# Recurrence of a hybrid block on one core: the next group's triangular inverse moved to a lower priority band, and another order and length of the filling projections

## The chip, the cores and the metric

The kernel runs on 1 core of one Trainium2 chip. The time is device microseconds (us) from launch to end, the median of several runs; lower is better. Engines are named as the profile names them: PE (TensorE), DVE (VectorE), ACT (ScalarE), POOL (GpSimd), SP (SyncE, which here only issues DMAs).

## The reference

Two layers of a block over 512 latent tokens and 256 context tokens, width 1024. In each layer one input projection of the normalised tokens feeds three mixers: a bidirectional RWKV-7 recurrence, multi-head latent attention, and windowed grouped-query attention (gqa). Each is multiplied by its own SiLU gate, projected, merged by sigmoid gates and passed through an output projection. The recurrence, as the reference states it:

```
def step(S, inp):
    r_t, w_t, k_t, v_t, kk_t, a_t = inp
    sa = jnp.einsum('bhvk,bhk->bhv', S, kk_t)
    S = (S * w_t[:, :, None, :] - sa[..., None] * (kk_t * a_t)[:, :, None, :]
         + v_t[..., None] * k_t[:, :, None, :])
    return S, jnp.einsum('bhvk,bhk->bhv', S, r_t)
```

It runs over 768 tokens, 8 heads of 64 channels, in both directions.

## The kernel before

**The recurrence.** It is done in chunks of 64 tokens: 12 steps, each of which handles 8 heads in both directions (16 pairs). Within a chunk the token-by-token rule becomes a triangular system, so each chunk needs the inverse of a unit lower triangular 64x64 matrix per pair. These inverses are made for a group of four steps at a time (`NS` 4, `NG` 3 groups; `rwkv_inverse`, L634-685). The matrices are loaded (tile TT, L641/642, issued on SP), turned with a stream transpose (L647), and the two 32x32 diagonal blocks are inverted on DVE by 30 pairs of a multiply (L657) and an add (L659), then turned back (L662, L663). PE then makes the block below the diagonal from two halves of matmuls: zp, yp, zp, yp. Of the tile TT and of its working tile `inv` there is one buffer each; of the result YB there are two.

A step (`rwkv_step`, L687-742) is a chain: PE makes Rp, ACT copies it, PE makes Up with the inverse, ACT and DVE copy it (L708, L709), PE makes Sp, DVE makes the new state So (L719, L720), which ACT and DVE copy for the next step (L694, L695). The scores of the chunk two steps ahead (`rwkv_scores`, L587-633: matmuls scps, DVE masks L623 and L625) are woven into the step, in two halves.

**The filling.** Since the chain leaves PE idle, the remaining tiles of the input projection are woven in. A tile is 128 output columns over eight blocks of 128 input channels; in single precision each product is three matmuls (`hh`x`wh`, `hl`x`wh`, `hh`x`wl`), for 512 latent tokens and, in layer 0, for 256 context tokens too. It is cut into 8 pieces; `pace(n)` emits n of them. `FILL` (L33) holds, per layer, how many stand before the first inverse, during it, in its last parts, and in the steps. The matmul results lie in two PSUM buffers (`g`, GB 2). A "raw" tile is copied out by ACT (L756); a "silu" tile (a gate) is evacuated by ACT's tanh (L758) and a DVE multiply (L760), both at the band SERVE. In layer 0 the woven work carries pieces of the next conditioning vectors along (modps, modpt; DVE L261, L269).

**What sets the order.** The program is emitted under priority bands, and a scheduler gives each engine one fixed order: SERVE first, then B+1 (steps, scores, inverses), B+3 (gqa tokens), B+4 (filling). PE's instructions of the recurrence and its filling are chained to the order in which they were written (`in_line`, L146-160). In the loop over steps the next group's inverse is a generator, `ahead`: one part of its DVE work after each of steps 0, 1 and 2 of a group, its matmuls within step 3.

Of the kernel before, what the change touches and what calls it, by code (L numbers as in the profile page):

```python
# [29 lines left out]
GB, RB, CB = 2, 3, 2  # L30


FILL = ((48, 36, 2, (2, 2, 2), (3, 3, 3), 2), (72, 56, 4, (2, 2, 2), (3, 3, 3), 2))  # L33

QUEUES = (("scalar", "sync", "sync", "scalar"), ("sync", "scalar", "sync", "sync"))

# [1 line left out]
NS, NG = 4, 3  # L38
# [22 lines left out]
def build(tc, A, out):  # L61
# [13 lines left out]
    @contextmanager  # L75
    def band(b):

        keep, mine = tc.cur_priority, bands.get(b, b * 1000000)
        tc.cur_priority = mine
        yield  # L80
        bands[b] = tc.cur_priority
        tc.cur_priority = keep
# [64 lines left out]
    @contextmanager  # L147
    def in_line():
        line["on"] = True
        yield  # L150
        line["on"] = False
# [339 lines left out]
    def rwkv(l, D, last, DL, B, pace, zlast):  # L491

        with tc.tile_pool(name="rw", bufs=1, reuse_waits="tile") as rp:
            yo = rp.tile([P, 4, T], F32, name="yo")
            st = {"seen": set(), "S": None}
            parts, YB = {}, {}

            def scores(i):
                if i < NCH:
                    parts[i] = yield from rwkv_scores(l, last, rp, i)  # L500

            def invert(g):
                if g < NG:
                    YB[g] = rp.tile([P, 32, 64], F32, tag="YB", name="YB", bufs=2)
                    yield from rwkv_inverse(l, rp, g, YB[g])

            def rest(*gens):
                for g in gens:
                    for _ in g:
                        pass  # L510

            with band(B + 1):
                rest(scores(0), scores(1))
                ahead = invert(0)
                for _ in range(3):
                    next(ahead)
            with band(B + 4), tc.issue_after(zlast):
                pace(FILL[l][1])
            with band(B + 1), in_line():
                for _ in ahead:  # L520
                    pace(FILL[l][2])
                ahead = out = iter(())
                for i in range(NCH):
                    if i % NS == 0:
                        rest(ahead)
                        ahead = invert(i // NS + 1)
                    nxt = scores(i + 2)
                    step = rwkv_step(l, last, i, yo, st, DL, rp, parts.pop(i), YB[i // NS])
                    for n in FILL[l][3 if i % NS < NS - 1 else 4]:
                        next(step, None)  # L530
                        next(nxt, None)
                        if i % NS == NS - 1:
                            next(ahead, None)
                        next(out, None)
                        pace(n)
                    rest(step, nxt)
                    if i % NS < NS - 1:
                        next(ahead, None)
                    if i in READY and (i > 3 or not last):
                        rest(out)  # L540
                        out = readout(l, D, rp, yo, READY[i])
                for _ in out:
                    pace(FILL[l][5])

    def readout(l, D, rp, yo, part):

        b, t = part

        def cols(a):
            a = a.rearrange("p (b t) -> p b t", t=T // 2)[:, b, t]  # L550
            return a if len(a.shape) == 3 else a.unsqueeze(1)

        def like(a, y):
            return a.rearrange("p (b t) -> p b t", b=y.shape[1])

        tmp = rp.tile([P, 6, 256], F32, tag="AR", name="ro", bufs=4)
        def spread(p):
            ps = psum_bcast(256)
            mm(ps, bones, tmp[:, 4 + p % 2])
            V.tensor_scalar(tmp[:, p], ps, 1.0 / 64, None, ALU.mult)  # L560

        for p in range(4):
            y = cols(yo[:, p])
            ps = psum_bcast(256)
            mm(ps, C["center"], y)
            S.copy(y, like(ps, y))
            S.activation(like(tmp[:, 4 + p % 2], y), y, AF.Square)
            if p:
                spread(p - 1)
            yield  # L570
        spread(3)
        var = tmp[:, 0:4]
        S.activation(var, var, AF.Ln, bias=b_gn)
        S.activation(var, var, AF.Exp, scale=-0.5)
        for p in range(4):
            y = cols(yo[:, p])
            ro = rp.tile([P, 2, 256], F32, tag="UV", name="ro2", bufs=4)
            bv, gt = like(ro[:, 0], y), like(ro[:, 1], y)
            DMA.dma_start(bv, cols(bv_d[l][p]))
            DMA.dma_start(gt, cols(g_d[l][p]))  # L580
            V.scalar_tensor_tensor(y, y, D["gng"][:, p:p + 1], like(tmp[:, p], y), ALU.mult, ALU.mult)
            V.scalar_tensor_tensor(y, y, D["gnb"][:, p:p + 1], bv, ALU.add, ALU.add)
            V.scalar_tensor_tensor(y, gt, 0.5, y, ALU.mult, ALU.mult)
            DMA.dma_start(cols(yg_d[l][p]), y)
# [160 lines left out]
    def proj(l, hh, hl, j, dst, segs, kind, side):  # L745

        t = spool.tile([P, T], F32, tag="st", name="st", bufs=2)
        if j == T_KR:
            ps = yield from narrow_steps(A["w_in"][l][j], KT, hh, hl, segs, side)
        else:  # L750
            ps = yield from gemm_steps(A["w_in"][l][j], KT, hh, hl, segs, "gg", side)
        with band(SERVE):
            for (s0, n), p in zip(segs, ps):
                sl = slice(s0, s0 + n)
                if kind == "raw":
                    S.copy(t[:, sl], p)  # L756
                else:
                    S.activation(t[:, sl], p, AF.Tanh, scale=0.5)  # L758
                    if kind == "silu":
                        V.scalar_tensor_tensor(t[:, sl], t[:, sl], 1.0, p, ALU.add, ALU.mult)  # L760
            s0 = segs[-1][0]
            DMA.dma_start(dst[:, s0:T], t[:, s0:T])
# [653 lines left out]
    for l in range(2):  # L1416
        last = l == 1
# [3 lines left out]
        B = 10 * l  # L1421
# [22 lines left out]
        def tiles():  # L1444

            zb = [(T_CQ + j, zb_d[l][j], (LAT,) if last and j < 2 else BOTH, "raw") for j in range(4)]
            zc = [(T_ZC + j, zb_d[l][4 + j], (LAT,) if last and j < 4 else BOTH, "raw") for j in range(6)]
            ga, gb, gc = ([(t + j, g_d[l][4 * n + j], segs, "silu") for j in range(4)]
                          for n, t in enumerate((T_GA, T_GB, T_GC)))
            todo = zb[2:] + zc[4:] + zc[:4] + zb[:2] + ga + gb if last else zb + ga + gb + zc  # L1450
            todo += gc + [(T_ZG + j, th_zg[l][j], segs, "tanh") for j in range(24)]
            for a in todo:
                yield from proj(l, hh, hl, *a, side)
                yield

        steps = tiles()

        def pace(n):

            for _ in zip(range(n), steps):  # L1460
                pass
# [3 lines left out]
        with band(B + 4):  # L1465
            pace(FILL[l][0])
        ss = cpool.tile([P, 6, 10], F32, tag="ss", name="ss")
        if last:
            cctx.close()
            with band(B + 3):  # L1470
                gqa_tokens(l, F, last, ss)
        rwkv(l, D, last, DL, B, pace, zlast)
        weights["queue"] = getattr(nc, QUEUES[l][2])
        with band(B + 4), tc.issue_after(line["last"]):
            pace(22 * 8 - sum(FILL[l][0:2]) - 2 * FILL[l][2] - NG * (3 * sum(FILL[l][3]) + sum(FILL[l][4])) - 4 * FILL[l][5])

# [162 lines left out]
```

## Time and profile before

| | us |
|---|---|
| median of 3 runs (lowest to highest) | 2433.22 (2431.24 to 2439.78) |
| profiled execution | 2433.78 |
| span of its trace | 2432.1 |
| PE busy | 2166.8 (89%) |
| DVE busy | 1278.8 (53%) |
| ACT busy | 894.1 (37%) |
| POOL busy | 844.3 (35%) |

The span runs from the first to the last instruction of the trace; 1.7 us of the execution lie around it. Times in the trace count from the span's start. Layer 0's recurrence takes from about 325 us to 675, layer 1's from about 1650 to 1945. A busy share is an average over all of the kernel; within the recurrence PE and DVE take turns at being waited for.

### The profile page before, as it was taken

The page shows a single profiled execution, that of the slowest core. Times are in us where ns is not written, and L with a number is a line of the kernel's source. Part 1 is how long each engine was busy: PE and PEld are TensorE (multiplying, and loading weights), DVE is VectorE, ACT ScalarE, POOL GpSimd, SP SyncE. Part 2 cuts the span into 40 slices and gives each one's busy share as a digit, 9 for nine tenths or more (in the row PEclk, how much of TensorE's full clock was granted, in tenths as well). Part 3 has the DMA queues.
Part 4 walks back from the last instruction along what each step waited for, and adds up shares of the span by engine and source line. Part 5 has one row for each costly group of instructions (what it writes and reads, how often), then busy time and mean ns, then how long its engine had stood idle before and what let it go on. Part 6 is the DMA issues. An engine that isn't in the chain of part 4 may idle for free. (4 is left out here: it accounts for less than half of the span.)

```text
span 2432.1 us, 42833 instructions
## 1 busy us (share of the span) xinstructions
PE 2166.8 (89%) x16824; PEld 1657.7 (68%) x16824; DVE 1278.8 (53%) x2300; ACT 894.1 (37%) x1654; POOL 844.3 (35%) x699
## 2 busy tenths in 40 slices
PE   7988895888998999899989998798968998999989
PEld 4766683667877666766767786666756876666667
DVE  5466326865347663466145356736577456545223
ACT  4443221223354333543222345332322465334322
POOL 1244221111123444444333224443211144454464
PEclk9998997998999999999999999899988999999989
DMA  7146665445251013511685314665553262011474
GB/s 251 61 137 195 199 198 129 127 127 140 73 176 50 20 53 95 172 36 47 217 269 172 122 61 125 180 194 160 134 124 88 90 208 87 18 52 36 139 248 159
DMA packets 330442, 314.25 MB, mean 129 GB/s; under 512 B 112768, under 2 KB 239488, under 8 KB 330240
## 3 DMA queue, kind: packets, MB, share of 16 engines
q1 hardware_dynamic: 315120, 283.97, 39.2%
q10 hardware_dynamic: 15120, 27.53, 3.5%
q8 instruction: 133, 2.18, 0.4%
q14 instruction: 69, 0.57, 0.1%
HBM read 213.64 MB, written 97.78 MB: 128 GB/s over the span
## 5 line engine op out<-in xcount | busy, mean ns | idle before, releaser
L166 POOL TENSOR_TENSOR wl<-wf,wh 128x512 fp32r<-128x512 f32 x316 | 426.1, 1350 | 1060.1 <-ACT wh L165 979.9
L154 PE MATMUL g<-hh,wh 128*128 128x512 f32 (+1 forms) x1264 | 467.1, 370 | 14.1 <-DVE st L760 11.2
L154 PE MATMUL g<-hh,wl 128*128 128x512 f32 (+1 forms) x1264 | 457.0, 362 | 1.5 <-POOL wl L166 1.5
L154 PE MATMUL g<-hl,wh 128*128 128x512 f32 (+1 forms) x1264 | 454.1, 359 | 0.0
L165 ACT CAST wh<-wf 128x512 fp32r<-128x512 f32 x316 | 195.2, 619 | 503.4 <-PE g L154 233.8
L154 PEld LDWEIGHTS g<-hh,wh 128*128 128x128 f32 x1264 | 247.8, 196 | 66.4 <-issue 14.9
L154 PEld LDWEIGHTS g<-hh,wl 128*128 128x128 f32 x1264 | 247.7, 196 | 43.0 <-issue 9.4
L154 PEld LDWEIGHTS g<-hl,wh 128*128 128x128 f32 x1264 | 248.7, 197 | 38.7 <-issue 10.1
L867 POOL TENSOR_TENSOR acc<-acc,pe 128x512 f32<-128x512 f32 (+2 forms) x128 | 146.3, 1143 | 144.6 <-ACT pe L863 135.0
L863 ACT ACTIVATE pe<-stp 128x256 f32<-128x256 f32 (+2 forms) x224 | 114.5, 521 | 201.7 <-PE stp L154 194.9
L845 DVE TENSOR_REDUCE mx<-mps 128x1 f32<-128x384 f32 (+2 forms) x256 | 127.8, 535 | 68.7 <-PE mps L154 66.4
L154 PE MATMUL yps<-pe,vh 128*64 128x256 f32 (+1 forms) x704 | 132.5, 386 | 0.0
L154 PE MATMUL g<-yh,wh 128*128 128x512 f32 (+1 forms) x224 | 84.8, 384 | 21.9 <-DVE zt L1349 11.0
L1349 DVE SCALAR_TENSOR_TENSOR zt<-zt,g 128x512 f32<-128x512 f32 (+1 forms) x56 | 32.0, 576 | 129.8 <-PE g L154 86.6
L659 DVE TENSOR_TENSOR YB<-YB,inv 128x30 f32<-128x30 f32 (+9 forms) x180 | 91.9, 511 | 5.3
L657 DVE TENSOR_TENSOR inv<-inv,YB 128x30 f32<-128x30 f32 (+9 forms) x180 | 87.8, 488 | 8.9 <-issue 2.8
L154 PE MATMUL g<-yl,wh 128*128 128x512 f32 (+1 forms) x224 | 85.2, 384 | 6.3 <-POOL yl L1334 6.2
L154 PE MATMUL gc<-hh,wh 128*128 128x512 f32 x192 | 79.1, 412 | 7.8 <-ACT hh L325 4.5
L758 ACT ACTIVATE st<-g 128x256 f32<-128x256 f32 (+1 forms) x108 | 56.6, 524 | 76.0 <-PE g L154 66.4
L623 DVE TENSOR_TENSOR AR<-scps,cst 64x256 f32<-64x256 f32 x96 | 40.1, 418 | 82.2 <-PE scps L154 81.1
L154 PE MATMUL g<-yh,wl 128*128 128x512 f32 (+1 forms) x224 | 82.1, 371 | 0.0
L154 PE MATMUL gc<-hl,wh 128*128 128x512 f32 x192 | 79.5, 414 | 0.0
(395 smaller groups left out, 4402.0 us busy)
## 6 DMA issues: line engine op xcount, KB each, us to landing
wf<-w_in SPq DMA_DIRECT2D x159, 256.0 KB, 3.0
wf<-ada_w SPq DMA_DIRECT2D x96, 256.0 KB, 3.7
wf<-w_in ACTq DMA_DIRECT2D x81, 256.0 KB, 3.0
bkd<-bk SPq DMA_DIRECT2D x16, 768.0 KB, 5.2
zt<-thzg SPq DMA_DIRECT2D x48, 256.0 KB, 3.8
wf<-w_bo SPq DMA_DIRECT2D x40, 256.0 KB, 3.3
thzg<-st SPq DMA_DIRECT2D x24, 384.0 KB, 2.3
md<-zt SPq DMA_DIRECT2D x32, 256.0 KB, 3.5
```

The lines of the kernel that those rows point to most:

```text
L154: queued(TE.matmul(o, l, r, start=start, stop=stop, **kw))
L165: S.copy(wh, w32)
L166: eng.tensor_tensor(wl, w32, wh.bitcast(F32), ALU.subtract)
L623: V.tensor_tensor(AR[oth, pds, 2 * par, :], ps[oth, :, a0:a0 + 64], msk("ms", oth), ALU.mult)
L657: V.tensor_tensor(t3, M3[:, 0:j, j:j + 1].to_broadcast([P, j, n]), Y3[:, j:j + 1, j + 1:32].to_broadcast([P, j, n]), ALU.mult)
L659: V.tensor_tensor(Y3[:, 0:j, j + 1:32], Y3[:, 0:j, j + 1:32], t3, ALU.add)
L758: S.activation(t[:, sl], p, AF.Tanh, scale=0.5)
L845: V.tensor_reduce(mx, ps, AX.X, ALU.max)
L863: S.activation(e, st, AF.Exp, scale=scale)
L867: G.tensor_tensor(acc, keep.pop(0, acc), e, ALU.add)
L1349: V.scalar_tensor_tensor(th, th, 1.0, p_, ALU.add, ALU.mult)
```

## The change

Three edits. The next group's inverse is started at the group's first step, all of its DVE work at once, in a band of its own (B+2) between the steps and the filling; the calls that did a part after each step go. In layer 0 the six copied tiles `zc` come right after the four `zb`, ahead of the gates `ga` and `gb`. And the pieces of filling during the first inverse grow from 36 to 64 in layer 0 and from 56 to 60 in layer 1.

```diff
-FILL = ((48, 36, 2, (2, 2, 2), (3, 3, 3), 2), (72, 56, 4, (2, 2, 2), (3, 3, 3), 2))
+FILL = ((48, 64, 2, (2, 2, 2), (3, 3, 3), 2), (72, 60, 4, (2, 2, 2), (3, 3, 3), 2))
...
                 for i in range(NCH):
                     if i % NS == 0:
                         rest(ahead)
+
                         ahead = invert(i // NS + 1)
+                        with band(B + 2):
+                            for _ in range(3):
+                                next(ahead, None)
...
                     rest(step, nxt)
-                    if i % NS < NS - 1:
-                        next(ahead, None)
...
-            todo = zb[2:] + zc[4:] + zc[:4] + zb[:2] + ga + gb if last else zb + ga + gb + zc
+            todo = (zb[2:] + zc[4:] + zc[:4] + zb[:2] if last else zb + zc) + ga + gb
```

Lines of the changed kernel stand 2 further down in these functions (L647 is L649, L663 is L665, L760 is L762).

DVE, layer 0, where the inverse of the second group begins. Before, it begins right after the state of step 0 (So, UV) and the masks of a later step's scores (L623, L625) come in between its pairs:

```order
L722 TENSOR_TENSOR So<-Sp,DL 128x512
L695 COPY UV<-So 64x512
L647 STREAM_TRANSPOSE inv<-TT 128x1024
L760 SCALAR_TENSOR_TENSOR st<-st,g 128x512
L261 COPY row<-modps 128x256
L653 MEMSET YB 128x32
L657 TENSOR_TENSOR inv<-inv,YB 128x30
L659 TENSOR_TENSOR YB<-YB,inv 128x30
```

Now it begins after the first masks within step 3 (the So and UV ahead of them are those of step 2):

```order
L722 TENSOR_TENSOR So<-So,DL 128x512
L697 COPY UV<-So 64x512
L741 TENSOR_TENSOR yo<-yo,Yp 128x4x64 x2
L762 SCALAR_TENSOR_TENSOR st<-st,g 128x512
L625 TENSOR_TENSOR AR<-scps,cst 64x4x64
L627 TENSOR_TENSOR TR<-scps,cst 128x4x64
L625 TENSOR_TENSOR AR<-scps,cst 64x4x64
L627 TENSOR_TENSOR TR<-scps,cst 128x4x64
L649 STREAM_TRANSPOSE inv<-TT 128x1024
L655 MEMSET YB 128x32
L659 TENSOR_TENSOR inv<-inv,YB 128x30
L661 TENSOR_TENSOR YB<-YB,inv 128x30
```

All 30 pairs then follow one another with nothing between them, up to the two transposes, and the copy of step 3's Up comes behind. What has moved is the whole inverse, from steps 0 to 2 into step 3; layer 1's stands alike, with 24 operations of gqa's tokens (three sets for q, three for k) among its pairs. On SP the last two of the four loads of TT for this group, which stood ahead of the loads for the scores of step 3, now stand behind those of BK for step 7.

PE in step 3 of layer 0, first before, then now: zp, which reads the inverse, is the third thing in the step in both.

```order
L154 MATMUL Rp<-UV,AR 64x64 x16
L154 MATMUL scps<-AR,BK 128x128 x8
L154 MATMUL zp<-inv,TT 32x32 x32
L154 MATMUL g<-hh,wh 128x256
L154 MATMUL g<-hl,wh 128x256
L154 MATMUL g<-hh,wl 128x256
```

```order
L154 MATMUL Rp<-UV,AR 64x64 x16
L154 MATMUL scps<-AR,BK 128x128 x8
L154 MATMUL zp<-inv,TT 32x32 x32
L154 MATMUL g<-hh,wh 128x256
L154 MATMUL g<-hl,wh 128x256
L154 MATMUL g<-hh,wl 128x256
```

PE's order around zp has not moved; what stands on DVE ahead of the result that it reads has.

DVE in layer 0's first inverse, its end. Before, the pairs run out without a gate's evacuation between them:

```order
L657 TENSOR_TENSOR inv<-inv,YB 128x58
L659 TENSOR_TENSOR YB<-YB,inv 128x2x29
L657 TENSOR_TENSOR inv<-inv,YB 128x30
L659 TENSOR_TENSOR YB<-YB,inv 128x30
L662 STREAM_TRANSPOSE YB<-YB 128x32x32
L663 STREAM_TRANSPOSE inv<-YB 128x1024
L760 SCALAR_TENSOR_TENSOR st<-st,g 128x512
```

Now the evacuations (L762) of the third gate tile stand at the very end, one within the last pair and one behind the transposes, and the fourth's behind those:

```order
L661 TENSOR_TENSOR YB<-YB,inv 128x2x29
L659 TENSOR_TENSOR inv<-inv,YB 128x30
L762 SCALAR_TENSOR_TENSOR st<-st,g 128x256
L661 TENSOR_TENSOR YB<-YB,inv 128x30
L664 STREAM_TRANSPOSE YB<-YB 128x32x32
L665 STREAM_TRANSPOSE inv<-YB 128x1024
L261 COPY row<-modps 128x256
L762 SCALAR_TENSOR_TENSOR st<-st,g 128x512
L272 TENSOR_TENSOR mod_162<-modpt,pp 128x4
L762 SCALAR_TENSOR_TENSOR st<-st,g 128x256
```

The first two gate tiles' evacuations stand after the 7th, after the 10th, in the 18th and after the 20th pair; PE has 3.5 tiles more ahead of the first zp than before.

## Rows read from the trace of the kernel before

**Rows 1.** The page: the span, and the busy time of each engine.
```profile
span 2432.1 us, 42833 instructions
PE 2166.8 (89%) x16824; PEld 1657.7 (68%) x16824; DVE 1278.8 (53%) x2300; ACT 894.1 (37%) x1654; POOL 844.3 (35%) x699
```

**Rows 2.** Waits of PE, 370 to 425 us: us in total, times, longest.
```profile
PE zp L154 <- DVE inv L663: 29.7, 1, 29.7
```

**Rows 3.** Timeline of DVE, layer 0's first inverse: start, duration, operation, [idle before].
```profile
372.61 2.01 DVE L647 STREAM_TRANSPOSE inv<-TT 128x1024 f32<-128x1024 f32 x1
...
380.29 0.41 DVE L760 SCALAR_TENSOR_TENSOR st<-st,g 128x256 f32<-128x256 f32 x1
...
394.96 0.55 DVE L657 TENSOR_TENSOR inv<-inv,YB 128x234 f32<-128x234 f32 x1
...
408.99 1.25 DVE L663 STREAM_TRANSPOSE inv<-YB 128x1024 f32<-128x1024 f32 x1
```

**Rows 4.** Timeline of PE, the first zp of two groups.
```profile
410.29 1.92 PE L154 MATMUL zp<-inv,TT 32*32 32x32 f32 x64 [29.73 <-DVE inv L663]
...
490.42 1.20 PE L154 MATMUL zp<-inv,TT 32*32 32x32 f32 x64
```

**Rows 5.** Windows: stretch, length; busy PE, PEld, DVE, ACT, POOL; PEclk, DMA, GB/s.
```profile
400.00:420.00 20.00, 9.71 (x222) 7.76 (x223) 11.29 (x23) 6.19 (x9) 3.02 (x3) 0.63 0.17 50
...
1180.00:1190.00 10.00, 6.54 (x18) 4.48 (x18) 0.00 (x0) 3.38 (x7) 6.63 (x7) 0.66 0.83 259
```

**Rows 6.** Timeline of DVE: evacuations of two gate tiles that follow each other.
```profile
357.47 0.42 DVE L760 SCALAR_TENSOR_TENSOR st<-st,g 128x256 f32<-128x256 f32 x1 [2.58 <-ACT st L758]
...
367.52 0.42 DVE L760 SCALAR_TENSOR_TENSOR st<-st,g 128x256 f32<-128x256 f32 x1 [2.56 <-ACT st L758]
```

**Rows 7.** Timeline of PE, layer 0: Rp of steps 0, 3, 4, 8 and 9.
```profile
421.82 1.15 PE L154 MATMUL Rp<-UV,AR 128*64 128x64 f32 x32
...
486.94 1.98 PE L154 MATMUL Rp<-UV,AR 128*64 128x64 f32 x32
...
513.98 1.15 PE L154 MATMUL Rp<-UV,AR 128*64 128x64 f32 x32
...
613.42 1.15 PE L154 MATMUL Rp<-UV,AR 128*64 128x64 f32 x32
...
628.63 1.09 PE L154 MATMUL Rp<-UV,AR 128*64 128x64 f32 x30
```

**Rows 8.** Timeline of DVE: last mask of the first half of step 0's scores.
```profile
425.21 0.41 DVE L625 TENSOR_TENSOR TR<-scps,cst 128x256 f32<-128x256 f32 x1
```

**Rows 9.** Timelines of SP's queue and of DVE: the second group's load, what waits for it.
```profile
432.05 0.56 SPq L642 DMA_DIRECT2D TT<-ttd  x1
...
487.69 0.59 SPq L592 DMA_DIRECT2D BK<-bkd  x1
...
435.92 2.01 DVE L647 STREAM_TRANSPOSE inv<-TT 128x1024 f32<-128x1024 f32 x1 [1.41 <-DMA TT<-ttd]
```

**Rows 10.** Timeline of PE, layer 1: Rp of steps 0, 1, 4; zp in step 3.
```profile
1731.00 1.15 PE L154 MATMUL Rp<-UV,AR 128*64 128x64 f32 x32
...
1741.71 1.15 PE L154 MATMUL Rp<-UV,AR 128*64 128x64 f32 x32
...
1790.54 1.92 PE L154 MATMUL zp<-inv,TT 32*32 32x32 f32 x64 [13.83 <-DVE inv L663]
...
1809.84 1.15 PE L154 MATMUL Rp<-UV,AR 128*64 128x64 f32 x32
```

**Rows 11.** Lines of DVE, 1650 to 1990 us, gqa's tokens: xcount | busy, mean ns | idle before.
```profile
L1166 DVE TENSOR_REDUCE ss<-x 128x2 f32<-128x128 f32 (+1 forms) x10 | 4.4, 442 | 15.5 <-ACT x L1165 15.4
L1140 DVE TENSOR_TENSOR rp<-gqm,scq 128x256 f32<-128x256 f32 x8 | 3.0, 413 | 0.0
L1136 DVE TENSOR_TENSOR x<-gqm,ccq 128x512 f32<-128x512 f32 x4 | 2.8, 691 | 0.5 <-DVE ss L1166 0.4
L1140 DVE TENSOR_TENSOR rp<-gqm,sck 128x64 f32<-128x64 f32 x8 | 1.5, 214 | 0.0
```

## The prediction

> **What bounds the kernel now.** I began with the page's busy times [rows 1]: PE at 89% is the engine that fills the span, so outside the recurrence nothing here can move much. Next, PE's waits by stretch. The largest single one in the recurrences is in layer 0: the first zp waits 29.7 us for the first inverse [rows 2]. The timelines show why. DVE starts that inverse at 372.61 and is done at 410.24 (408.99 and 1.25) [rows 3], PE ran out of filling at 380.56 (410.29 less 29.73) [rows 4]. Some 36 us of the 37.6 are the inverse itself, the rest other small operations: this is the price of an inverse that DVE does in one piece.
>
> The second inverse of layer 0 is the opposite case: begun at 435.92 [rows 9], spread over steps 0 to 2, and finished in time, so that its zp at 490.42 carries no wait [rows 4]. It costs something all the same: from Rp of step 0 to Rp of step 4 pass 92.2 us (421.82 to 513.98), where step 8, with no inverse beside it, takes 15.2 [rows 7]. In layer 1 the same stretch takes 78.8 us (1731.00 to 1809.84) against 10.7 for step 0, and there zp in step 3 waits 13.8 [rows 10].
>
> **The change part by part.** The sum is made against the profiled execution, 2433.8, which is 0.6 above the median of the runs.
>
> *Layer 0's first inverse.* The change puts 28 more pieces, 3.5 tiles, ahead of the first zp. A tile with its riders takes 10.05 us here (357.47 to 367.52) [rows 6], so PE has 35 us for a hole of 29.7, and if nothing else were in the way, all of the hole would go. Something is. Four of the tiles there are now gates, whose results leave PSUM by DVE, in DVE's fixed order among the pairs, and PE has two buffers. Before, the same tile that is now the first gate had its context half evacuated at 380.29 [rows 3]; the next one's is ready 10 us later, near 390.5. Its place on DVE, though, is in the 18th pair (394.96 before), so with the two evacuations ahead of it about 397, and PE, ready for the third gate at about 391.5, loses some 6 us. The third's place is in the last pair: 407 plus four evacuations, about 409 to 410. The fourth can't begin before that, and its second half not before the evacuation behind the transposes, about 415. PE is then at zp near 425, with 35 us more done than before at 410.3: it lost 10 to 12 us on the way, where it lost 29.7. I take 11. To this comes the slow restart: after the wait zp took 1.92 us, elsewhere 1.20 [rows 4], and the granted clock in 400 to 420 was 0.63 [rows 5]; I put that at 2. Gain 29.7 - 11 + 2 = **21**; bounds 32 (no such coupling) and 10 (it costs twice as much).
>
> *Layer 0, second inverse.* The lower band doesn't lay it between the steps. By the order, none of its DVE work comes before the masks in step 3, then all of it comes in one piece, and zp on PE is right behind. PE then has nothing it may do. Steps 0 to 2 go undisturbed, 15.2 each, 45.5 in all. In step 3 the masks end 3.8 us after Rp (425.21 + 0.41 against 421.82) [rows 7, 8], then 36 us of inverse, then what followed zp before, 23.6 (490.42 to 513.98). One more wait: the inverse needs TT. SP's queue got to the loads for the next scores about 0.8 us into step 3 (487.69), and the last load of TT landed some 5.4 us after its issue at 432.05 (DVE waited for it until 435.92, an estimate of 3.9 for issue and landing) [rows 9]; the last two loads of TT are now queued behind those, so I add 4 us (0 to 8). Sum 45.5 + 3.8 + 4 + 36 + 23.6 = 112.9, against 92.2: **+21** (13 to 27). The restart at half clock is in it only as far as it was before (Rp of step 3 took 1.98 instead of 1.15).
>
> *Layer 1, second inverse.* The same, with gqa's three q and three k sets on DVE among the pairs. A set of each is two reductions of 0.44, 0.69 and 0.29 for the products, two times 0.41 and two times 0.21 [rows 11] (the 0.29 is an estimate: a little under 0.69 x 0.21/0.41), 3.1 us, three times 9.4. Steps 0 to 2: 3 x 10.7, and 1 for gqa there, 33. Step 3: 3.8 + 1 for TT + 36 + 9.4 + 19.3 (1790.54 to 1809.84, which has the slow clock in it) = 69.5. Together 102.5 against 78.8: **+24** (14 to 30).
>
> *Third inverses.* They begin within step 4 instead of just ahead of it, mixed with the steps' own work as before, since by then the steps are held by the readout and by the masks. Same DVE work, same steps beside it: 0 in layer 0 (-4 to 4), +2 in layer 1 (0 to 4).
>
> *The rest.* Copies ahead of gates take DVE work from before the first inverse to among its pairs, which is priced above; ACT, at 37% [rows 1], does either kind. The gates that the first readout reads are done 116 pieces in, 112 are needed, so no wait there. Layer 1's four further pieces stand where PE had work anyway: 0. Where layer 0's filling ends, fewer pieces are left, and the merge's first matmuls now come before gqa's last; in 1180 to 1190 PE was busy 6.54 of 10 us at a clock of 0.66 [rows 5], so -4 (-8 to 0).
>
> Sum: -21 + 21 + 24 + 0 + 2 - 4 = +22, that is 2455.8; less the 0.6 to the median, **2455 us**.
>
> A rule that bears on the clock term: the Trainium skill, "TensorE: Matmul & The Clock Gate", section "HAM oscillation — how this bites in real kernels", says that an engine that falls idle between bursts pays a cold start at each return. By it the change swaps one such return for another: layer 0's first inverse loses its own, step 3 gains one, and the 2 us credited above would be given back; the sum would be 24 instead of 22. The trace agrees that the return is slow (1.92 against 1.20), and doesn't show what a wait in step 3 of layer 0 does.
>
> **The rivals.**
>
> *Faster: the band does what it says in the last groups.* If steps 4 to 7 run first and the third inverse fills their holes only, these steps, 99.4 us from Rp of step 4 to that of step 8 (513.98 to 613.42) [rows 7], come down toward 3 x 15.2 + 23.6 = 69.2. That is 30 us in layer 0, and layer 1's group, an estimate from the same ratio, 20. With all of it the sum is 22 - 50 = -28, 2405; it decides for faster from 30 of the 50 on. For it: the inverse begins later than before, after step 4's masks. Against it: DVE's work between step 4 and step 7 is the same, and the steps on PE need DVE's masks and copies that stand behind the pairs.
>
> *Within 0.3%: the first hole goes entirely and the lumps cost less.* If evacuations find DVE in time (-32), TT lands early (+17) and gqa's sets slip into the wait without lengthening it (+15), the sum is -32 + 17 + 15 + 2 - 4 = -2, 2431. For it: a hole of 29.7 for 35 us of filling. Against it: PSUM has two buffers and DVE one order.
>
> *Slower still.* PE loses in the first inverse twice what I took (-10), the TT loads come at the late end (+27), layer 1's chain of gqa waits for its transposes on a PE that stands at zp (+30): -10 + 27 + 30 + 4 = +51, 2484.
>
> *That the change does nothing where it says so* would need an order like before; the order shows the inverses moved, so this holds only if the steps wait for something else at the same places. It ends with the second rival.
>
> **How the numbers follow.** The forecast has 0.62 (its own range 2442 to 2468, all slower), the faster rival 0.13, the same-time rivals 0.16, the slower still 0.09. What a measurement here tells from no change is about 0.3%, 7.3 us: 2425.9 to 2440.5. So slower 0.62 + 0.09 = 0.71, within 0.16, faster 0.13. The range of 8 in 10 leaves out most of the faster rival and of the slower one: 2428 to 2474.
>
> **What would show it.** In the profile after: in layer 0 the wait of the first zp for L665 shrunk to a few us, with waits of the filling's g for L762 in its place, 6 to 12 us in all; in step 3 of layer 0 a wait of zp for L665 of about 37 to 41 us, and in layer 1 of 40 to 50; steps 0 to 2 at about 15 and 11 us; the clock at 0.6 or so behind both waits; the stretch of steps 4 to 7 within 4 us of 99. The forecast is wrong if these two waits are not there or are under 25 us each, if steps 4 to 7 come down by more than 10 us, or if the first inverse's gain is given back by its evacuations.

## The result and the profile after

The changed kernel takes 2489.76 us (2486.84 to 2492.06, 4 runs) against 2434.3 before (2431.24 to 2439.78, 4 runs): a ratio of 1.0236, 95% interval 1.0213 to 1.0258. It was forecast slower, and is, but by 55 us where 21 were forecast; 2489.76 lies outside the range of 2428 to 2474.

The page of the changed kernel, span and busy times (they answer to [rows 1]): the work is the same (as many matmuls and DVE operations), the span 57.7 us longer, so PE waits more.

```profile
span 2489.8 us, 42818 instructions
PE 2163.9 (87%) x16824; PEld 1648.5 (66%) x16824; DVE 1279.9 (51%) x2300; ACT 894.2 (36%) x1654; POOL 840.2 (34%) x699
```

PE's timeline of the changed kernel in layer 0 (start, duration, operation, [idle before]): the first zp, Rp of steps 0 and 3, zp of step 3, Rp of steps 4 and 8; they answer to [rows 4, 7].

```profile
434.38 1.20 PE L154 MATMUL zp<-inv,TT 32*32 32x32 f32 x64
...
444.81 1.15 PE L154 MATMUL Rp<-UV,AR 128*64 128x64 f32 x32
...
492.19 1.15 PE L154 MATMUL Rp<-UV,AR 128*64 128x64 f32 x32
539.00 1.24 PE L154 MATMUL zp<-inv,TT 32*32 32x32 f32 x39 [44.57 <-ACT YB L667]
562.86 1.15 PE L154 MATMUL Rp<-UV,AR 128*64 128x64 f32 x32
...
656.60 1.15 PE L154 MATMUL Rp<-UV,AR 128*64 128x64 f32 x32
```

The wait of 29.73 us ahead of the first zp is gone; in step 3 one of 44.57 stands. The same in layer 1, Rp of steps 0, 3 and 4 and zp of step 3, which answer to [rows 10]:

```profile
1748.32 1.15 PE L154 MATMUL Rp<-UV,AR 128*64 128x64 f32 x32
...
1781.94 1.15 PE L154 MATMUL Rp<-UV,AR 128*64 128x64 f32 x32 [0.65 <-ACT UV L696]
...
1835.16 1.92 PE L154 MATMUL zp<-inv,TT 32*32 32x32 f32 x64 [9.36 <-DVE inv L665]
...
1855.69 1.15 PE L154 MATMUL Rp<-UV,AR 128*64 128x64 f32 x32
```

From Rp to zp of step 3 pass 53.2 us; the waits of PE in 1781 to 1836 us show that gqa's few transposes stand in between and split the wait in parts:

```profile
PE gqm L157 <- issue: 29.4, 3, 13.7
PE zp L154 <- DVE inv L665: 9.4, 1, 9.4
PE gqm L157 <- ACT x L1171: 8.0, 2, 4.3
```

Why DVE is late in step 3, in the changed kernel's timelines of DVE and of SP's queue: the last mask, the second inverse's begin, the same in layer 1; then the issues of TT in layer 0 (compare [rows 9]).

```profile
495.57 0.40 DVE L627 TENSOR_TENSOR TR<-scps,cst 128x256 f32<-128x256 f32 x1
503.83 1.90 DVE L649 STREAM_TRANSPOSE inv<-TT 128x1024 f32<-128x1024 f32 x1 [7.86 <-DMA TT<-ttd]
...
1792.82 1.91 DVE L649 STREAM_TRANSPOSE inv<-TT 128x1024 f32<-128x1024 f32 x1 [7.08 <-DMA TT<-ttd]
```

```profile
485.38 0.63 SPq L644 DMA_DIRECT2D TT<-ttd  x1
...
495.86 0.55 SPq L594 DMA_DIRECT2D BK<-bkd  x1
...
497.78 0.63 SPq L643 DMA_DIRECT2D TT<-ttd  x1
498.46 0.61 SPq L644 DMA_DIRECT2D TT<-ttd  x1
```

The last two loads of TT go out behind those of BK for a later step, at 498, where before they went out at 432 at the latest. DVE is free from 495.97, and waits 7.86 us for them.

PE's clock in two windows of that stretch (columns as in [rows 5]): half speed, and no matmul in the first.

```profile
500.00:520.00 20.00, 0.00 (x0) 0.00 (x0) 13.79 (x31) 0.00 (x0) 1.27 (x1) 0.50 0.15 22
520.00:540.00 20.00, 1.00 (x39) 1.03 (x40) 17.76 (x34) 2.08 (x2) 0.94 (x1) 0.50 0.00 0
```

Where the 57.7 us of span come from, by the distance between the same matmuls in both traces:

| stretch | before, us | after, us | difference |
|---|---|---|---|
| start to Rp of step 0, layer 0 | 421.8 | 444.8 | +23.0 |
| steps 0 to 3, layer 0 | 92.2 | 118.1 | +25.9 |
| steps 4 to 7, layer 0 | 99.4 | 93.7 | -5.7 |
| steps 8 to 10 | 44.7 | 44.7 | 0.0 |
| Rp of step 11 to the first zp of layer 1 | 1062.7 | 1036.8 | -25.9 |
| from there to Rp of step 0, layer 1 | 10.2 | 10.2 | 0.0 |
| steps 0 to 3, layer 1 | 78.8 | 107.4 | +28.5 |
| steps 4 to 10, layer 1 | 117.8 | 120.5 | +2.8 |
| Rp of step 11, layer 1, to the end | 504.5 | 513.6 | +9.1 |

One trace fixes such a stretch to a few us only: experiment 5 leaves layer 0 as it was, and in its trace the start is 3.1 us longer, steps 0 to 7 are 1.6 longer and the stretch from Rp of step 11 to Rp of step 0 in layer 1 is 3.7 shorter than before.

### The profile page after: what moved, and what is told of

It is laid out like the page before. It is cut to its first block, busy times and chain, and to the rows that moved or that the text cites. A ratio compares the mean times of both kernels' runs of the same rounds, so it can differ in the third digit from the quotient of the medians.

```text
span 2489.8 us, 42818 instructions
## 1 busy us (share of the span) xinstructions
PE 2163.9 (87%) x16824; PEld 1648.5 (66%) x16824; DVE 1279.9 (51%) x2300; ACT 894.2 (36%) x1654; POOL 840.2 (34%) x699
## 5 line engine op out<-in xcount | busy, mean ns | idle before, releaser
L154 PEld LDWEIGHTS g<-hh,wh 128*128 128x128 f32 x1264 | 247.9, 196 | 71.0 <-DVE st L762 17.7
L154 PEld LDWEIGHTS g<-hh,wl 128*128 128x128 f32 x1264 | 247.0, 195 | 45.5 <-issue 11.7
L154 PEld LDWEIGHTS g<-hl,wh 128*128 128x128 f32 x1264 | 248.6, 197 | 40.7 <-issue 11.8
L661 DVE TENSOR_TENSOR YB<-YB,inv 128x30 f32<-128x30 f32 (+9 forms) x180 | 97.0, 539 | 5.1
L625 DVE TENSOR_TENSOR AR<-scps,cst 64x256 f32<-64x256 f32 x96 | 40.1, 417 | 105.4 <-PE scps L154 104.4
L760 ACT ACTIVATE st<-g 128x256 f32<-128x256 f32 (+1 forms) x108 | 56.6, 524 | 64.3 <-PE g L154 54.6
```

The source lines that it names most:

```text
L154: queued(TE.matmul(o, l, r, start=start, stop=stop, **kw))
L625: V.tensor_tensor(AR[oth, pds, 2 * par, :], ps[oth, :, a0:a0 + 64], msk("ms", oth), ALU.mult)
L661: V.tensor_tensor(Y3[:, 0:j, j + 1:32], Y3[:, 0:j, j + 1:32], t3, ALU.add)
```

## The experiments

Each time is given with that of before from the same runs. Theory L: not the band of DVE's work, but the loads of TT, which are issued in it too, make the inverse late. Theory D, the prediction's: the band of the DVE work puts the inverse last.

**1. The change without its band** (FILL and the order of the tiles as in the change, the rest as before).

> The change without its band: copies first, 64 and 60 pieces during the first inverse, the next group's inverse spread over steps 0 to 2 as before. Theory A (PE's idle time in the first inverse is what the longer filling is worth, and all of it stays): the changed kernel's trace has 19.7 us less idle in that stretch than before, so about 2434 - 20 = 2414. Theory B (what the first hole gives is given back where the filling ends, as the stretch from the recurrence of layer 0 to that of layer 1 has 3.4 us more idle and the end 8.7 more): 2434 - 20 + 12 = 2426 or more.

Measured: 2436.45 against 2431.49, ratio 1.0021 (1.0002 to 1.0039). The first hole is gone in this trace too and nothing came of it. Theory A is wrong. Theory B's "2426 or more" holds, but its sum of 2426 is 10 us short; experiment 5 shows what that sum left out.

**2. The loads of TT back in the steps' band.** The substitution stays in B+2, at once.

```diff
-                for _ in range(3):
+                for _ in range(4):
                     next(ahead)
...
             DMA.dma_start(TT[b0 + 32:b0 + 64, :, :, 0:32], tt_d[l][b0 + 32:b0 + 64, :, cs, 32:64])
+        yield
...
+                        next(ahead, None)
                         with band(B + 2):
```

> The change with one thing undone: the four loads of TT for the next group are issued in the steps' band B+1, at the group's first step, and only the DVE work of the inverse stays in the lower band B+2. Theory L (the loads, queued on SP behind later scores, make the inverse late; the DVE band matters little): the two waits of zp in step 3 (44.6 us in layer 0, some 50 in layer 1) go and the time comes within 0.5% of the kernel without the band, near 2415 to 2425. Theory D (the lower band of the DVE work itself puts the inverse last): only the waits for the load go, 7.9 and 7.1 us, so 2490 - 15 = 2475.

Measured: 2429.83 against 2431.49, ratio 0.9996 (0.998 to 1.0012): 57 us under the changed kernel, each against its own before. That is above theory L's 2415 to 2425, because experiment 1 is no faster either, but both waits for the loads are gone and theory D's 2475 is far off. PE's timeline, zp of step 3 in layer 0 and in layer 1:

```profile
514.87 1.20 PE L154 MATMUL zp<-inv,TT 32*32 32x32 f32 x64
...
1779.33 0.87 PE L154 MATMUL zp<-inv,TT 32*32 32x32 f32 x25 [13.92 <-issue]
```

No wait in layer 0; in layer 1 the 13.9 us of before. On DVE the scheduler again puts the inverse right behind step 0's state, and mixes it with the steps, although its band is the lower one (it begins at 462.34, before Rp of step 1 at 464.21):

```order
L699 COPY UV<-So 64x512
L272 TENSOR_TENSOR mod_162<-modpt,pp 128x4
L651 STREAM_TRANSPOSE inv<-TT 128x1024
L657 MEMSET YB 128x32
L661 TENSOR_TENSOR inv<-inv,YB 128x30
L663 TENSOR_TENSOR YB<-YB,inv 128x30
```

**3. Only the loads in the lower band**, everything else as in experiment 1.

```diff
-                for _ in range(3):
+                for _ in range(4):
                     next(ahead)
...
             DMA.dma_start(TT[b0 + 32:b0 + 64, :, :, 0:32], tt_d[l][b0 + 32:b0 + 64, :, cs, 32:64])
+        yield
...
                         ahead = invert(i // NS + 1)
+                        with band(B + 2):
+                            next(ahead, None)
```

> The kernel without the band, but with the four loads of TT in the lower band B+2; the DVE work of the inverse stays in B+1, spread over steps 0 to 2 as before. Theory L: as slow as the changed kernel, 2485 to 2492, with zp waiting over 40 us in step 3 of both layers. Theory D: as fast as the kernel without the band, 2415 to 2426, but for a wait for the load of under 10 us.

Measured: 2485.37 against 2431.49, ratio 1.0226 (1.0199 to 1.0253). The two waits are back, with the DVE work in the steps' own band, zp of step 3 in both layers (in layer 1 gqa's transposes split the wait again: from Rp to zp pass 53.5 us, in the changed kernel 53.2):

```profile
537.63 1.92 PE L154 MATMUL zp<-inv,TT 32*32 32x32 f32 x64 [44.79 <-ACT YB L668]
...
1828.97 1.92 PE L154 MATMUL zp<-inv,TT 32*32 32x32 f32 x64 [9.36 <-DVE inv L666]
```

On DVE the inverse stands in one piece behind step 3's masks, as in the changed kernel, and waits there for TT:

```profile
502.50 1.90 DVE L650 STREAM_TRANSPOSE inv<-TT 128x1024 f32<-128x1024 f32 x1 [8.11 <-DMA TT<-ttd]
```

With 2 and 3 theory L is shown from both sides: the loads alone cost 48.9 us (2485.37 - 2436.45); the band of the DVE work alone gains 6.6 (2436.45 - 2429.83), which the spread of the runs leaves uncertain by some 4.

**4. The band alone**, FILL and tiles as before.

> The band edit alone: FILL and the order of the tiles as before, the next group's inverse started at once in band B+2, its loads too. In layer 1 the order puts the inverse in step 3 as in the changed kernel, in layer 0 it begins after step 1 and is mixed with two steps. Theory L with the end of layer 1 charged to the filling: layer 1 alone, 30 us more, layer 0 at most 10, nothing at the end: 2462 to 2472. If the 9 us at the end of layer 1 come of the band: 2472 to 2482. If layer 0's load waits as in the changed kernel: 2485.

Measured: 2470.03 against 2433.56, ratio 1.0148 (1.0131 to 1.0165). In layer 1 the wait is that of the changed kernel (zp at 1829.04, 53.3 us behind Rp at 1775.72); in layer 0 it is shorter. There the last load of TT went out at 446.94, and the inverse began at 452.10 without waiting for it:

```profile
497.75 1.92 PE L154 MATMUL zp<-inv,TT 32*32 32x32 f32 x64 [12.91 <-DVE inv L664]
```

From Rp of layer 1's step 11 to the end pass 504.4 us (1969.11 to 2473.5), as before: the 9 us at the end are not the band's. The time lies in the first of the three ranges.

**5. Four pieces in layer 1 alone** (`(72, 60, 4, ...)` in before).

> Before with one number changed: 60 instead of 56 pieces during layer 1's first inverse. Theory E (those four pieces are missing behind the recurrence, where the traces of all kernels with 60 have 7 to 9 us more idle): 5 to 10 us slower than before, 2437 to 2442. Theory N (the pieces change nothing, the end is longer by something of layer 0's): within 2 us of before.

Measured: 2448.89 against 2433.56, ratio 1.006 (1.0046 to 1.0074): 15.3 us for one number, more than theory E's 5 to 10. The end is 11.8 us longer (2443.5 - 1927.20 against 504.5), and all of it is idle time of PE (49.9 us there, 38.2 before). The timeline of DVE in this kernel, behind the last step:

```profile
1937.44 0.42 DVE L739 TENSOR_TENSOR yo<-yo,Yp 128x256 f32<-128x256 f32 x1 [3.07 <-PE Yp L154]
1938.56 0.88 DVE L581 SCALAR_TENSOR_TENSOR yo<-yo,pp,ro 128x256 f32<-128x256 f32 x2 [0.69 <-ACT ro L574]
...
1943.41 0.74 DVE L583 SCALAR_TENSOR_TENSOR yo<-ro,yo 128x256 f32<-128x256 f32 x2
1944.08 0.41 DVE L739 TENSOR_TENSOR yo<-yo,Yp 128x256 f32<-128x256 f32 x1
```

The two adds of the last result (L739) are torn apart: six pairs of another readout's operations stand between. PE needs the second for the last readout's first matmul:

```profile
1944.55 1.22 PE L154 MATMUL pr<-yo,cst 128*128 128x256 f32 x2 [4.65 <-DVE yo L739]
```

Before, both adds come together at 1937.89 and pr waits for nothing. The rest of the loss follows behind it, in the latent attention's start, as waits of a few us (4.1 for ACT's cqh, 2.8 for gqa's copies); I did not take those apart. The wait of pr for yo is no accident of this kernel: it stands, 4.6 to 4.9 us long, in the traces of all seven kernels with 60 or 52 pieces, the changed one among them, and in none of the six with 56. The end lasts 513 to 520 us in the seven and 504 to 505 in the six. The changed kernel's:

```profile
1993.58 1.22 PE L154 MATMUL pr<-yo,cst 128*128 128x256 f32 x2 [4.84 <-DVE yo L741]
```

**6. Gates first** in layer 0 (`ga + zb + zc + gb`), with the change's 64 and 60 pieces and without the band, so that all tiles during the first inverse are copied by ACT.

> As the kernel without the band, but in layer 0 the four gate tiles ga come first, then all ten copied tiles, so that no gate is evacuated by DVE between the pairs of the first inverse. Theory A: the 10 us of PE idle that the gates' evacuations cost there (waits of PE for L762's results) go too, so 8 to 12 us less than the kernel without the band, about 2404. Rival: PE idles there for other reasons (weights, riders' waits for DVE's copies) and the time is the same within 4 us.

Measured: 2426.55 against 2431.49, ratio 0.9987 (0.997 to 1.0004), 9.9 under experiment 1, as theory A forecast. The first zp comes at 425.49 instead of 433.85. But theory A's reason isn't what the trace shows: in experiment 1 only 2.8 us of PE's waits between 300 us and Rp of step 0 are for a gate's evacuation (L760). From the start to that Rp PE idles 54.1 us here and 58.9 there, and steps 0 to 7 are shorter as well (185.3 against 191.0). That the evacuations cost the 10 us is not shown.

**7. The same with 56 pieces in layer 1.**

> The kernel with gates first in layer 0 (64 pieces during the first inverse), with layer 1's pieces back at 56. Theory E: 5 to 10 us less than with 60, so 2417 to 2422, clearly under before. Theory N: 2426.

Measured: 2415.18 against 2433.56, ratio 0.9922 (0.9908 to 0.9936). With 5, the cost of the four pieces is had twice: 15.3 us there, and 13.4 here, each against its own before (18.4 under before with 56, 4.9 with 60).

**8. The riders stay** in the steps: `next(side, None)` does nothing during the 28 further pieces of experiment 7.

> As the last (gates first, 64 and 56), but the pieces of the next conditioning vectors (modps, modpt) don't ride along with the 28 further pieces of layer 0's first inverse; they stay in the steps behind it. Theory R (the steps 0 to 7 have PE time to spare for them, since they last as long without them, 191.0 against 191.6 us; ahead of the first zp the same work, some 7 us of PE, is on the path): first zp 7 to 10 us earlier, steps 0 to 7 as long, 2410 to 2414. Rival: PE waits for DVE at the first zp then, or the steps grow by as much: within 2 us of the last.

Measured: 2421.44 against 2433.56, ratio 0.994 (0.9925 to 0.9955), 6 slower than 7, with runs from 2412.9 to 2422.45 here and from 2411.79 to 2418.67 there. The first zp came no earlier (430.02, in 7 429.13), though PE did 72 fewer of the riders' matmuls ahead of it: PE waited 15.2 us for ACT to copy a tile out instead. ACT's timeline:

```profile
400.83 0.58 ACT L759 COPY st<-g 128x512 f32<-128x512 f32 x1
421.44 2.11 ACT L668 COPY YB<-YB 32x1024 f32<-32x1024 f32 x2 [20.03 <-DVE YB L665]
423.57 0.86 ACT L759 COPY st<-g 128x256 f32<-128x256 f32 x2
```

A copy of the inverse's own result stood ahead of the tile's copy in ACT's order, and ACT stood idle for 20 us until DVE had that result. PE had finished the tile at 408.8; its copy began at 423.57. So the run doesn't tell what the riders cost; its theory R got no support, and stays open.

**9. The change with both costs undone**: experiment 2 with 56 pieces in layer 1.

> The change with its two costs undone: the loads of TT in B+1 (its DVE work stays in B+2, at once) and 56 pieces in layer 1 as before. If the two are all that made the change slow, what is left of it: 2430 less the 12 to 15 us of layer 1's four pieces, 2415 to 2420, faster than before. Rival (layer 0's tail and gates keep it at the time of before): 2428 to 2434.

Measured: 2412.91 against 2431.29, ratio 0.9924 (0.9908 to 0.9939). That is a little under the 2415 to 2420 expected. Against the changed kernel it is 74 us, each against its own before, and with experiment 2 the four pieces are priced a third time: 16.7 us.

**10. The same with gates first.**

> The last with the gate tiles ga first in layer 0. If gates ahead of the copies and the lower band of the DVE work add (20 us without the band, 6 by the band in the other order): 2407 to 2411. Rival (the band's 6 us came of the gates' evacuations in the first inverse, so they are had once only): 2413 to 2419.

Measured: 2410.52 against 2431.29, ratio 0.9908 (0.9893 to 0.9923), the fastest here. It lies inside the first expectation's 2407 to 2411, by half a microsecond, and its interval overlaps that of 9: that the two gains add is not shown.

**11. 52 pieces in layer 1**, otherwise as 7.

> Gates first, 64 pieces in layer 0, and 52 instead of 56 pieces in layer 1's first inverse. If what 60 cost comes of fewer pieces left behind the recurrence (a slope): 2415 less up to 10, 2405 to 2412. If 60 stepped over an edge (the readout's first matmul then stands with nothing ahead of it while its state is being added): 52 is like 56, within 4 us of 2415, or slower by the clock or by an idle PE ahead of zp.

Measured: 2426.72 against 2431.29, ratio 0.9983 (0.9972 to 0.9994): 4.6 us under before, where 56 pieces are 18.4 under, so 13.8 slower. There is no slope, and the loss doesn't lie ahead of zp: Rp of step 11 comes 3.2 us earlier than in 7. Behind it the end lasts 519.8 us, in 7 503.9, and 10.8 of these 15.9 us are idle time of PE. The two adds are torn apart here too, and PE's other two waits of experiment 5 (4.1 and 2.8 us) are there again:

```profile
1923.32 1.22 PE L154 MATMUL pr<-yo,cst 128*128 128x256 f32 x2 [4.62 <-DVE yo L739]
```

So 52 and 60 both fall into the one order of the end, and 56 has the other, on which before's time rests.

## Why the prediction was wrong

By experiments 1 to 5 the 55 us divide so: four pieces in layer 1 +15 (5), the rest of the filling in layer 0 -10 (1 less 5, each against its own before, give or take 5), the late loads +49 (3 less 1), the band of the DVE work in the changed kernel about +2 (what is left). The forecast had 0, -25, and together +47 for the last two. So two of its steps failed, by 15 us each: the price of nothing for layer 1's four pieces, and the credit of 25 for layer 0's filling. They make up nearly all of the 34 us between forecast and measured. The forecast's terms beside the runs:

**"Layer 1's four further pieces stand where PE had work anyway: 0": the first step that failed.** They cost 15.3 us alone (5). I looked only at the place where the pieces were added; the loss lies behind the recurrence, where PE idles 11.7 us more. So the opening premise, that outside the recurrence nothing can move much, was wrong too. What the pieces moved was the order of everything behind, down to two adds on DVE behind the last step; that accounts for 4.7 of the 11.8 us at the end, and the rest is not taken apart.

**Layer 0's first inverse, -21, and -4 at the end of the filling: the second step that failed.** The wait at the first zp fell as forecast: from 300 us to Rp of step 0 PE idles 10.5 us in the changed kernel, 30.2 before (length of the windows less PE's busy time), where I took 11. The size is partly luck, for the gates' evacuations, which I forecast at 6 to 12, are the smaller part of it. The largest waits of PE in that window of the changed kernel follow; the first is for copies of the riders, which stand in DVE's order too:

```profile
PE modpt L154 <- DVE row L261: 5.1, 3, 2.1
PE g L154 <- DVE st L762: 2.8, 2, 1.7
```

Of the 19.7 us less idle some 10 reached the time by the medians; by the table above it was 3 (23.0 us later at Rp of step 0, 25.9 shorter behind step 11). I had priced the filling with its riders, 35 us for 28 pieces, as if all of it were to come back. Ahead of Rp of step 0 they kept PE busy for some 41 us (23.0 later, with 17.7 less idle from the start on). Two places gave back less. In steps 0 to 7 the riders that PE now does ahead of zp were missing, but with experiment 1's undisturbed order these steps last 191.0 us, before 191.6: the waits for riders (10.7 us before) went, and others came in their place, 10.3 us for loads of AR (before 4.4) and 11.7 for DVE's masks (before 3.4). And at the end of the filling, Rp of step 11 to layer 1 became 22.2 us shorter in experiment 1, where 28 pieces without riders are 29.4 (an estimate from 8.4 us a tile); in the first 120 us behind the steps PE idles 5 us more. With gates first, that stretch is 29.3 shorter, and the kernel with 56 pieces is 18 us faster than before (experiment 7).

**Second inverses, +45 forecast (21 and 24): mechanism and size near, the cause named too broadly.** That the inverse would come in one piece in step 3, with PE standing at zp, is what the traces show: 44.6 us in layer 0, 53.2 from Rp to zp in layer 1. Layer 0's sum with measured terms is 47.4 + 3.8 + 7.9 + 35.2 + 23.9 = 118.1, where 112.9 was forecast: most of the difference is the wait for TT behind the masks, 7.9 us (in layer 1 7.1), where I took 4 and 1. (The term gives the landing of TT twice, as 5.4 and as 3.9 us; [rows 9] have 3.9.) But "the lower band doesn't lay it between the steps" blames the wrong half: the DVE work in the lower band is laid between them when its loads are early (2), and with only the loads in that band it stands behind step 3's masks (3), which costs 49 us. How the scheduler comes to that order, no run shows; my reading is that it goes by when it thinks the data will be there. I had the loads in my hands, as 4 us of landing, and took them for an addition where they were the whole. As for the slow return behind the wait, the stretch from zp of step 3 to Rp of step 4 in layer 0 is 23.9 us, before 23.6.

**Third inverses: 0 and 2 forecast, -5.7 and 2.8 measured.** Layer 1's is inside its bounds; layer 0's is outside (-4 to 4), but experiment 1, whose third inverse stands as before, has -4.7 there, so most of it is not the inverse's doing. The rival that these steps would come down by 30 us didn't happen.

Of the rivals, "slower still" at 2484 was nearest in time, and half of its mechanism came true: its loads at the late end (8 us, 7.9 measured) and its gqa on a waiting PE give +27 and +30 for the second inverses, 25.9 and 28.5 measured. Its third part, a first inverse that gains half, came about in size, but not by the evacuations. The four pieces were in no rival.

## What to carry to other kernels

A lower priority band holds for all that is emitted in it: the loads as well as the arithmetic. Issue the loads for deferred work at the band of what must be on time, and defer only the arithmetic; here that is the difference between 2490 and 2430 us. When a filling is moved, count separately what it costs in front and what it gives back behind; in the changed kernel's trace the two were 41 us of PE's time and 26. A few pieces of filler more or less are not free even where they are hidden: look, in the order of the engines, at what stands behind them, and measure the neighbours of a tuned number.

## What the runs showed that was not expected

Two neighbours of one count, 52 and 60 pieces against 56, are both slower by 13 to 17 us, with the same operations on every engine. And an engine that only copies can be the one that holds PE: ACT, at 36 to 37%, copied a finished tile nearly 15 us late, because a copy queued ahead of it waited for DVE (8). In the changed kernel the long wait of zp in layer 0 is put down to ACT's copy of YB (44.57 <-ACT YB L667), which itself follows DVE's transposes.
